# A decoder layer on one core: the down projection's weight operands made one to three products later

## The chip, the core and the metric

The kernel runs on one core of a Trainium2 chip. The metric is the device time of one execution in microseconds (us). Its engines are PE (TensorE, matmuls), DVE (VectorE), ACT (ScalarE), POOL (GpSimd) and SP (SyncE, here only a DMA queue); each works through its own list of instructions in order, and they wait for one another by semaphores.

## What is computed

One decoder layer for 1056 positions (1024 of a prompt, 32 of samples), d_model 1024, all in float32:

```
x = x + 1/2 * SwiGLU_1(RMSNorm(x))          # (silu(h @ w_gate) * (h @ w_up)) @ w_down, d_ff 2816
z = RMSNorm(x) @ w_in                       # attention head group and short-conv head group
x = x + concat([attn_out, conv_out]) @ w_out
x = x + 1/2 * SwiGLU_2(RMSNorm(x))
x = x + sigmoid(RMSNorm(x) @ w_ple_gate) * (p @ w_ple_proj)
```

The change is in the product with `w_down`, which occurs twice (two down stages).

## The kernel before

**Precision.** Each float32 operand is held as a high part (a cast to the PE's reduced format, on ACT) and a low part (operand minus high part, on DVE); a product is three matmuls: high by high, low by high, high by low. `split` (L370 the cast, L371 the subtraction) makes both parts of one operand.

**Seven products.** Every 2x2 block product of the SwiGLU stages is done with seven products in place of eight; sums and differences of blocks are their operands. Products carry the numbers 1 to 7. The operands of the weights' side are 1, 2 and 4 (blocks as they are loaded, tiles `dr`) and 3, 5, 6, 7 (sums of blocks, tiles `dws`, which POOL makes in four additions, L829 to L832, in the order of operands 5, 6, 7, 3). `vh` and `vl` are the high and the low part, one place of each for every operand number: the parts of the next weights overwrite those in use, so they can be made only when the product that reads them is done.

**Flushes.** A down stage is 17 flushes (table `FLUSH`): one row of weights, one to three pairs of d_ff blocks, added to x. The positions come in two chunks, so each flush has two halves, called here the first half (chunk 0) and the second (chunk 1), with the same weights. A product in a half is three matmuls for each pair: three, six or nine.

**Order in a half.** `segment(q, p)` interleaves a half with the late products of the half before it. The seven steps are products 1, 5 of this half, 7 of the previous, 2, 6 of this, 3, 4 of the previous. After each product `out1` to `out7` take the sum from PSUM into x ("puts": L871 on DVE; L869 on ACT for part of the puts of flushes that begin with pair 0). After product 1 one put, after 5 none, after 7 two, after 2, 6, 3 and 4 one each. Products 1, 6, 7 and 4 of a half add up in one PSUM bank, 5 and 3 in a second, 2 alone in a third; there are five banks. Two waits follow: product 3 may add to its bank only after the second put of product 7 has read it, two steps after product 7; and product 5 of a half takes the bank that product 3's put of the half before it has emptied, two steps after that product.

**Who sets the order.** From the end of the gate-up stage to the end of the down stage the order on each engine is as written (`in_order`). In the second half of each flush, `follow` holds the next weights, and `step` splits operand o of them right after product o of the flush in use and its put. The additions for them (`sums`) stand at the start of the second half on POOL, whose list also holds the loads of the pairs' operands (L907) and the additions of the residual (L914, two in eight of the flushes). Flushes 5 and 6 also make the last pair's operands (`hop_last`, tiles `hd`, `hta`, `htb`, `hhi`, `sgl`), one task after each step.

In the program's steps:

```
            self.product(o, ps, o in (1, 5, 2))
            getattr(self, f"out{o}")()
            if self.follow:
                self.follow.split(o)
```

Of the kernel before, what the change touches and what calls it, by code (L numbers as in the profile page):

```python
# [78 lines left out]
FLUSH = [  # L79
    (0, 0, 1), (1, 0, 2), (2, 0, 2), (3, 0, 3), (0, 1, 4), (1, 2, 5), (2, 2, 5), (3, 3, 6), (0, 4, 7),  # L80
    (1, 5, 8), (2, 5, 8), (3, 6, 9), (0, 7, 9), (1, 8, 11), (2, 8, 11), (3, 9, 11), (0, 9, 11),
]
# [19 lines left out]
def tile_decoder_layer(  # L102
# [17 lines left out]
    def at(name, o, n, dt=F32, rows=P):  # L120

        assert o + n <= ARENA
        key = (name, o, n)
        if key not in placed:
            placed[key] = nc.alloc_sbuf_tensor_at(f"{name}_a{o}", [P, n], dt, offset=base + 4 * o).ap()
        return placed[key][:rows]
# [14 lines left out]
    def psb(pool=None):  # L141
        return (pool or mm).tile([P, 512], F32, name="ps", tag="ps")
# [27 lines left out]
    def pump_dma():  # L170
        while st["dma"] < st["end"] and st["dma"] < st["split"] + RAW:
            i = st["dma"]
            t = at("wraw", 30624 if i in (0, 26) else (URAW2 if 4 <= i < 26 else URAW)[i % 2], 1024)
            nc.sync.dma_start(out=t, in_=units[i])
            raws[i] = t
            st["dma"] += 1

    def split_one():
        i = st["split"]
        pump_dma()  # L180
        raw = raws.pop(i)
        hi = at("whi", unit_at(i), 1024, F32R)
        lo = at("wlo", unit_at(i) + 1024, 1024, F32R)
        nc.scalar.copy(out=hi, in_=raw)
        nc.vector.tensor_tensor(out=lo, in0=raw, in1=hi.bitcast(F32), op=ALU.subtract)  # L185
        parts[i] = (hi, lo)
        st["split"] += 1
        pump_dma()
# [174 lines left out]
    OPS = (1, 5, 2, 6, 7, 3, 4)  # L363
# [12 lines left out]
    def wload(gu, j):  # L376
        r = []
        for i in range(4):
            t = at("wr", WRAW + 512 * (wn_[0] % 6), 512)
            wn_[0] += 1  # L380
            nc.sync.dma_start(out=t, in_=gu[j, i])
            r.append(t)
        return r
# [4 lines left out]
    class Weights:  # L388


        def __init__(self, gu, j):
            r = wload(gu, j)
            s = [at("ws", WS + 512 * i, 512) for i in range(4)]
            add = nc.gpsimd.tensor_tensor
            add(out=s[0], in0=r[2], in1=r[3], op=ALU.add)  # L395
            add(out=s[1], in0=s[0], in1=r[0], op=ALU.add)
            add(out=s[2], in0=r[0], in1=r[2], op=ALU.add)
            add(out=s[3], in0=s[1], in1=r[1], op=ALU.add)
            self.of = {1: r[0], 2: r[1], 3: s[3], 4: r[3], 5: s[0], 6: s[1], 7: s[2]}
            self.w = {}  # L400
# [35 lines left out]
    class Quad:  # L436


        pops = 2

        def __init__(self, w, c):
            self.w, self.ch, self.follow = w, c, None

            self.then = {}
# [11 lines left out]
        def step(self, o):  # L456
            if o == 1:
                self.b = psb()
            elif o == 5:
                self.c = psb()  # L460
            elif o == 2:
                self.a = psb()
            ps = self.b if o in (1, 6, 7, 4) else self.c if o in (5, 3) else self.a
            self.product(o, ps, o in (1, 5, 2))
            getattr(self, f"out{o}")()
            if self.follow:
                self.follow.split(o)
            for fn in self.then.get(o, ()):
                fn()
            for _ in range(self.pops):  # L470
                if hops:
                    hops.pop(0)()

    hops = []

    def segment(q, p):

        for o, of in ((1, q), (5, q), (7, p), (2, q), (6, q), (3, p), (4, p)):
            if of:
                of.step(o)  # L480
# [60 lines left out]
    def hop_last(pr, c, src):  # L541


        cell = {}
        e0 = at("sgl", LASTAT, HH, F32R)

        def parts(u, n, hi, t, neg=False):
            split(hi, t.bitcast(F32R), t, neg)
            for part, v in enumerate((hi.bitcast(F32), t)):
                if n == 1:  # L550
                    nc.sync.dma_start(out=hop[pr, u, :, part * HC + c * HH:part * HC + (c + 1) * HH], in_=v)
                else:
                    nc.sync.dma_start(out=hop_dst(pr, c, u, n, part), in_=v)

        new = lambda: wtile("hhi", shape=[P, 2, HH], dt=F32R)
        return hop_sums(cell, src) + [
            lambda: parts(1, 2, new(), cell["s"][1]),
            lambda: parts(0, 1, e0, cell["s"][0][:, 0]),
            lambda: parts(3, 2, new(), cell["a"]),
            *[lambda: None] * 5,  # L560
            lambda: parts(5, 2, new(), cell["b"], True),
        ]
# [6 lines left out]
    def from_hd(pr, c):  # L569
        t = [tmp3("hd0"), tmp3("hd1")]  # L570
        for i in range(2):
            nc.sync.dma_start(out=t[i].rearrange("p i t -> p (i t)"), in_=hd[(2 * pr + i) % 16, :, c * HC:(c + 1) * HC])
        return lambda: t
# [171 lines left out]
    def gate_up(gu, g, lw, steps, down):  # L745
# [11 lines left out]
        n1 = len(bg)  # L757
        lead[1] = lead_weights(gu, 1)
        run(0, 0, -(-n1 // 8))
        run(1, 0, -(-n1 // 8))  # L760
        while bg:
            bg.pop(0)()
# [3 lines left out]
        for kp in range(2):  # L766
            bg.append(lambda kp=kp: n_t5(1, kp))
        run(0, 1)
        lead[2] = lead_weights(gu, 2)
        run(1, 1)  # L770
# [73 lines left out]

    class DownQuad(Quad):
        pops = 1

        def __init__(self, w, c, flush, done):
            super().__init__(w, c)
# [48 lines left out]
    class Down:  # L898
# [26 lines left out]
        def run(self, prev):  # L925
            w = self.w[0]
            last_use = {}
            for i, (row, p0, p1) in enumerate(FLUSH):
                for pr in range(p0, p1):
                    last_use[pr] = i  # L930
            last_row = {f[0]: i for i, f in enumerate(FLUSH)}
            for i, f in enumerate(FLUSH):
                nxt = None
                for c in range(2):
                    if c and i + 1 < len(FLUSH):
                        nxt = self.w[i + 1]
                        nxt.sums()
                    done = (lambda r=f[0], c=c: self.hook(r, c)) if last_row[f[0]] == i and f[0] else None
                    q = DownQuad(w, c, f, done)
                    if c:  # L940
                        q.follow = nxt
                        if i in (0, 2):
                            for o in UNITS:
                                q.then[o] = [lambda pr=2 + i // 2, o=o: self.load(pr, o)]
                        for pr in range(f[1], f[2]):
                            if last_use[pr] == i and pr + 4 < PAIRS:
                                for o in UNITS:
                                    q.then.setdefault(o, []).append(lambda pr=pr, o=o: self.load(pr + 4, o))
                    if i in (4, 5) and c:
                        src = from_hd(10, i - 4)  # L950
                    if i in (5, 6) and c == 0:
                        hops.extend(hop_last(10, i - 5, src))
                    if i == len(FLUSH) - 1 and c:
                        q.then[2] = [split_one]
                    if c == 0:
                        res = [self.residual(m, RES[i][1]) for m in (RES[i][0], RES[i][0] + 4)] if i in RES else []
                    else:
                        for fn in res:
                            fn()
                    segment(q, prev)  # L960
                    prev = q
                    if c and i + 2 < len(FLUSH):
                        self.w[i + 2] = self.weights(i + 2)
                    if (i, c) in ((len(FLUSH) - 2, 1), (len(FLUSH) - 1, 0)):
                        st["end"] = self.end - 3 * c
                        pump_dma()
                w = nxt
            segment(None, prev)
            self.hook(0, 0)
            split_one()  # L970
            self.hook(0, 1)
# [172 lines left out]
    for h in range(8):  # L1144
        o = h * TBL
# [586 lines left out]
```

## Time and profile before

| | |
|---|---|
| median of 3 runs | 2020.54 us (2017.55 to 2022.1) |
| the profiled execution | 2018.56 us, its span 2016.8 us |
| granted clock, mean over the span | 0.984 of full speed |
| busy share of the span | PE 97%, DVE 68%, POOL 46%, ACT 38% |
| matmuls of the two down stages | 2 x 1848 (L860 to L862) |
| casts and subtractions for the down weights | 238 each |

PE is busy nearly throughout. A row of a timeline shows in brackets how long the engine was idle before it, and what ended that.

### The profile page before, as it was taken

The numbers are of one execution on the slowest core, as the hardware profiler recorded it, in microseconds if no ns is written. First come the engines' busy times: TensorE is split into PE (matmuls) and PEld (weight loads), VectorE is DVE, ScalarE is ACT, GpSimd is POOL, SyncE is SP. The second block draws the span as 40 slices with busy tenths as digits, with TensorE's granted clock in tenths as the row PEclk, the third lists the DMA queues.
The fourth block names the chain that finished last, engine by engine and source line by source line (L and its number), as shares of the span: only waits on it lengthen the run. The fifth ranks groups of instructions, "written<-read, shape, count | busy, mean of one in ns | idle before, by whom it ended". The sixth has DMA issues, their size and how long they took to land. (4 is left out here: it accounts for less than half of the span.)

```text
span 2016.8 us, 38417 instructions
## 1 busy us (share of the span) xinstructions
PE 1947.3 (97%) x14639; PEld 1892.7 (94%) x14639; DVE 1378.3 (68%) x2572; ACT 770.8 (38%) x1654; POOL 918.1 (46%) x911
## 2 busy tenths in 40 slices
PE   7999999999999999999998899999999999999999
PEld 6999999999999998999886899999999999999898
DVE  6848877777577766366675367687777765777764
ACT  5324444444432234323343133344444434322431
POOL 2426654655566645012222025375565555675500
PEclk8999999999999999999998899999999999999999
DMA  7225754454999724201002321465444369876232
GB/s 253 74 75 194 246 167 139 136 163 135 316 321 322 252 81 152 68 23 43 26 29 75 117 97 54 140 221 169 134 156 160 124 216 326 295 262 233 67 111 88
DMA packets 189549, 315.47 MB, mean 156 GB/s; under 512 B 20801, under 2 KB 121545, under 8 KB 189236
## 3 DMA queue, kind: packets, MB, share of 16 engines
q1 hardware_dynamic: 164852, 224.55, 34.2%
q0 software_dynamic: 23648, 87.28, 12.8%
q8 instruction: 115, 1.88, 0.4%
q10 hardware_dynamic: 864, 1.18, 0.2%
q14 instruction: 70, 0.57, 0.1%
HBM read 204.66 MB, written 109.99 MB: 156 GB/s over the span
## 5 line engine op out<-in xcount | busy, mean ns | idle before, releaser
L452 PE MATMUL ps<-bh_a,wh_a 128*128 128x264 f32 x2128 | 603.3, 285 | 3.7 <-DVE u L604 1.8
L453 PE MATMUL ps<-bh_a,wl_a 128*128 128x264 f32 x2128 | 603.8, 284 | 0.0
L454 PE MATMUL ps<-bl_a,wh_a 128*128 128x264 f32 x2128 | 599.5, 284 | 0.0
L452 PEld LDWEIGHTS ps<-bh_a,wh_a 128*128 128x128 f32 x2128 | 399.1, 188 | 6.7 <-DVE g_a L607 2.5
L453 PEld LDWEIGHTS ps<-bh_a,wl_a 128*128 128x128 f32 x2128 | 400.0, 188 | 0.0
L454 PEld LDWEIGHTS ps<-bl_a,wh_a 128*128 128x128 f32 x2128 | 399.7, 189 | 0.0
L860 PE MATMUL ps<-pair_a,vh_a 128*128 128x264 f32 x1232 | 356.1, 289 | 25.8 <-DVE x_a L871 24.2
L862 PE MATMUL ps<-pair_a,vh_a 128*128 128x264 f32 x1232 | 351.8, 286 | 0.0
L861 PE MATMUL ps<-pair_a,vl_a 128*128 128x264 f32 x1232 | 350.9, 285 | 0.0
L860 PEld LDWEIGHTS ps<-pair_a,vh_a 128*128 128x128 f32 x1232 | 233.2, 189 | 34.0 <-ACT vh_a L370 12.3
L871 DVE SCALAR_TENSOR_TENSOR x_a<-ps,x_a 128x264 f32<-128x264 f32 x412 | 170.3, 426 | 104.2 <-PE ps L862 79.9
L861 PEld LDWEIGHTS ps<-pair_a,vl_a 128*128 128x128 f32 x1232 | 233.4, 189 | 0.0
L862 PEld LDWEIGHTS ps<-pair_a,vh_a 128*128 128x128 f32 x1232 | 232.7, 189 | 0.0
L342 PE MATMUL ps<-xnh_a,whi_a 128*128 128x384 f32 (+1 forms) x528 | 175.4, 332 | 9.4 <-DVE x_a L1551 6.0
L343 PE MATMUL ps<-xnh_a,wlo_a 128*128 128x384 f32 (+1 forms) x528 | 173.2, 328 | 1.6 <-DVE wlo_a L185 1.6
L344 PE MATMUL ps<-xnl_a,whi_a 128*128 128x384 f32 (+1 forms) x528 | 172.5, 327 | 0.0
L371 DVE TENSOR_TENSOR wl_a<-ws_a,wh_a 128x512 fp32r<-128x512 f32 x152 | 132.1, 869 | 35.9 <-ACT wh_a L370 35.5
L395 POOL TENSOR_TENSOR ws_a<-wr_a,wr_a 128x512 f32<-128x512 f32 x38 | 51.1, 1345 | 224.9 <-DMA wr_a<-in_w2gu_dram 88.4
L370 ACT CAST vh_a<-dws_a 128x384 fp32r<-128x384 f32 (+2 forms) x136 | 63.7, 468 | 201.0 <-PE ps L862 177.7
L370 ACT CAST wh_a<-ws_a 128x512 fp32r<-128x512 f32 x152 | 94.3, 620 | 101.4 <-PE ps L454 87.6
L907 POOL DMA_DIRECT2D pair_a<-hop x154 | 82.8, 544 | 84.0 <-PE ps L862 76.2
L371 DVE TENSOR_TENSOR wl_a<-wr_a,wh_a 128x512 fp32r<-128x512 f32 x114 | 108.1, 949 | 12.6 <-ACT wh_a L370 11.6
(268 smaller groups left out, 4177.3 us busy)
## 6 DMA issues: line engine op xcount, KB each, us to landing
pair_a<-hop POOLq DMA_DIRECT2D x154, 528.0 KB, 7.5
hop<-sg_a SPq DMA_DIRECT2D x240, 264.0 KB
wr_a<-in_w1gu_dram SPq DMA_DIRECT2D x88, 256.0 KB
wr_a<-in_w2gu_dram SPq DMA_DIRECT2D x88, 256.0 KB
hop<-sge_a SPq DMA_DIRECT2D x80, 132.0 KB
wraw_a<-in_win_dram SPq DMA_DIRECT2D x18, 512.0 KB
dr_a<-in_w1d_dram SPq DMA_DIRECT2D x44, 192.0 KB
dr_a<-in_w2d_dram SPq DMA_DIRECT2D x44, 192.0 KB
```

What stands on the lines that cost most here:

```text
L342: nc.tensor.matmul(ps[:, :W], lhsT=wh, rhs=xh, start=(k == 0), stop=False)
L343: nc.tensor.matmul(ps[:, :W], lhsT=wl, rhs=xh, start=False, stop=False)
L344: nc.tensor.matmul(ps[:, :W], lhsT=wh, rhs=xl, start=False, stop=(k == n - 1))
L370: nc.scalar.copy(out=hi, in_=src)
L371: nc.vector.tensor_tensor(out=lo, in0=src, in1=hi.bitcast(F32), op=ALU.subtract)
L452: nc.tensor.matmul(ps[:, :HH], lhsT=wh[:, ks], rhs=bh, start=(start and k == 0), stop=False, skip_group_check=True)
L453: nc.tensor.matmul(ps[:, :HH], lhsT=wl[:, ks], rhs=bh, start=False, stop=False, skip_group_check=True)
L454: nc.tensor.matmul(ps[:, :HH], lhsT=wh[:, ks], rhs=bl, start=False, stop=last, skip_group_check=True)
L860: nc.tensor.matmul(ps[:, :HH], lhsT=wh[:, ks], rhs=bh, start=(start and i == 0), stop=False, skip_group_check=True)
L861: nc.tensor.matmul(ps[:, :HH], lhsT=wl[:, ks], rhs=bh, start=False, stop=False, skip_group_check=True)
L862: nc.tensor.matmul(ps[:, :HH], lhsT=wh[:, ks], rhs=bl, start=False, stop=(i == n - 1), skip_group_check=True)
L871: nc.vector.scalar_tensor_tensor(out=x, in0=ps[:, :HH], scalar=f, in1=x, op0=ALU.mult, op1=ALU.add)
```

## The change

An operand's split is no longer called at once but put on a list, `behind`, with the number of the step at which it is due; the list is worked off in its order after each step's put. Outside the down stage the delay is 0 steps. In the down stage it is 1 step for operands 1, 7 and 3, 2 steps for 5, 2 and 4, and 3 for 6, but 0 for those of the last flush. Steps of the next half count, so operand 6, split after step 5 of the second half before, is split after step 1 of the next first half; 7 and 3 move within that half, to its steps 4 and 7; and operand 4 moves from its end to step 2 of the following second half, just ahead of operand 1 of the weights after.

```
@@ class Quad
+        behind = {o: 0 for o in OPS}
@@ Quad.step
             if self.follow:
-                self.follow.split(o)
+                behind.append((steps[0] + self.behind[o], lambda: self.follow.split(o)))
+            while behind and behind[0][0] <= steps[0]:
+                behind.pop(0)[1]()
+            steps[0] += 1
...
+    behind, steps = [], [0]
@@ class DownQuad(Quad)
+        behind = {1: 1, 5: 2, 2: 2, 6: 3, 7: 1, 3: 1, 4: 2}
@@ Down.run
+                    if i == len(FLUSH) - 2 and c:
+                        q.behind = Quad.behind
```

The lists of PE, POOL and SP hold the same instructions in the same order as before; those of ACT and DVE are in another order, with the same instructions.

In the listings, `x_a<-ps` is a put, and the low parts have the endings `vl_a_6049` operand 1, `6066` 5, `6105` 2, `6122` 6, `6188` 7, `6217` 3, `6235` 4. First DVE from the end of flush 12's first half to the start of flush 13, in the first down stage, before:

```order
L371 TENSOR_TENSOR vl_a_6217<-dws_a_6021,vh_a_6216 128x256
L871 SCALAR_TENSOR_TENSOR x_a_72<-ps,x_a_72 128x264
L371 TENSOR_TENSOR vl_a_6235<-dr_a_6291,vh_a_6234 128x256
L871 SCALAR_TENSOR_TENSOR x_a_72<-ps,x_a_72 128x264
L371 TENSOR_TENSOR vl_a_6049<-dr_a_6026,vh_a_6048 128x384
L371 TENSOR_TENSOR vl_a_6066<-dws_a_6018,vh_a_6065 128x384
L871 SCALAR_TENSOR_TENSOR x_a_72<-ps,x_a_72 128x264 x3
L371 TENSOR_TENSOR vl_a_6105<-dr_a_6028,vh_a_6104 128x384
L871 SCALAR_TENSOR_TENSOR x_a_72<-ps,x_a_72 128x264
L371 TENSOR_TENSOR vl_a_6122<-dws_a_6019,vh_a_6121 128x384
L871 SCALAR_TENSOR_TENSOR x_a_72<-ps,x_a_72 128x264 x5
```

and now:

```order
L371 TENSOR_TENSOR vl_a_6217<-dws_a_6021,vh_a_6216 128x256
L878 SCALAR_TENSOR_TENSOR x_a_72<-ps,x_a_72 128x264
L371 TENSOR_TENSOR vl_a_6235<-dr_a_6289,vh_a_6234 128x256
L371 TENSOR_TENSOR vl_a_6049<-dr_a_6026,vh_a_6048 128x384
L878 SCALAR_TENSOR_TENSOR x_a_72<-ps,x_a_72 128x264 x3
L371 TENSOR_TENSOR vl_a_6066<-dws_a_6018,vh_a_6065 128x384
L878 SCALAR_TENSOR_TENSOR x_a_72<-ps,x_a_72 128x264 x2
L371 TENSOR_TENSOR vl_a_6105<-dr_a_6028,vh_a_6104 128x384
L878 SCALAR_TENSOR_TENSOR x_a_72<-ps,x_a_72 128x264 x2
L371 TENSOR_TENSOR vl_a_6122<-dws_a_6019,vh_a_6121 128x384
```

Ahead of the row of three puts (7, 7, 2) of the second half stood 4, 1 and 5, and stand 3, 4 and 1; ahead of the put of product 3 (the last before `6122` moved away) stood 2 and 6 as well, and stands only 5.

DVE in the first half of flush 5, before (the first row ends with the two puts of product 7):

```order
L871 SCALAR_TENSOR_TENSOR x_a_72<-ps,x_a_72 128x264 x5
L371 TENSOR_TENSOR vl_a_6188<-dws_a_6020,vh_a_6187 128x384
L371 TENSOR_TENSOR hd_6812<-hd_6812,hhi 128x528
L871 SCALAR_TENSOR_TENSOR x_a_72<-ps,x_a_72 128x264
L371 TENSOR_TENSOR hd_6811<-hd_6811,sgl_a_6906 128x264
L871 SCALAR_TENSOR_TENSOR x_a_72<-ps,x_a_72 128x264
L371 TENSOR_TENSOR hta<-hta,hhi 128x528
L871 SCALAR_TENSOR_TENSOR x_a_72<-ps,x_a_72 128x264
L371 TENSOR_TENSOR vl_a_6217<-dws_a_6021,vh_a_6216 128x384
```

and now:

```order
L878 SCALAR_TENSOR_TENSOR x_a_72<-ps,x_a_72 128x264 x2
L371 TENSOR_TENSOR hd_6810<-hd_6810,hhi 128x528
L878 SCALAR_TENSOR_TENSOR x_a_72<-ps,x_a_72 128x264
L371 TENSOR_TENSOR vl_a_6188<-dws_a_6020,vh_a_6187 128x384
L371 TENSOR_TENSOR hd_6809<-hd_6809,sgl_a_6904 128x264
L878 SCALAR_TENSOR_TENSOR x_a_72<-ps,x_a_72 128x264
L371 TENSOR_TENSOR hta<-hta,hhi 128x528
L878 SCALAR_TENSOR_TENSOR x_a_72<-ps,x_a_72 128x264 x2
L371 TENSOR_TENSOR vl_a_6217<-dws_a_6021,vh_a_6216 128x384
```

The subtraction of operand 7 (`6188`) went from ahead of the first task on `hd` to behind it and the put that follows; operand 3's (`6217`) went behind one more put.

DVE in the second half of flush 0, before:

```order
L371 TENSOR_TENSOR vl_a_6235<-dr_a_5891,vh_a_6234 128x128
L371 TENSOR_TENSOR vl_a_6049<-dr_a_6026,vh_a_6048 128x256
L371 TENSOR_TENSOR vl_a_6066<-dws_a_6018,vh_a_6065 128x256
L871 SCALAR_TENSOR_TENSOR x_a_72<-ps,x_a_72 128x264 x2
L371 TENSOR_TENSOR vl_a_6105<-dr_a_6028,vh_a_6104 128x256
```

and now:

```order
L371 TENSOR_TENSOR vl_a_6235<-dr_a_5891,vh_a_6234 128x128
L371 TENSOR_TENSOR vl_a_6049<-dr_a_6026,vh_a_6048 128x256
L878 SCALAR_TENSOR_TENSOR x_a_72<-ps,x_a_72 128x264 x2
L371 TENSOR_TENSOR vl_a_6066<-dws_a_6018,vh_a_6065 128x256
L878 SCALAR_TENSOR_TENSOR x_a_72<-ps,x_a_72 128x264
```

Only operand 5 (`6066`) moved here, from ahead of the two puts (7 and 2) to behind them, since the operands split in the last gate-up step are not delayed.

## Rows read from the trace of the kernel before

**Rows 1.** Head of the page.

```profile
span 2016.8 us, 38417 instructions
```

**Rows 2.** Windows of the two down stages (busy us, instructions, granted clock, DMA).

```profile
517.00:768.00 251.00, 238.25 (x1889) 234.20 (x1889) 176.88 (x343) 83.63 (x187) 149.90 (x174) 0.99 0.73 248
1660.00:1910.00 250.00, 236.92 (x1898) 232.78 (x1897) 177.36 (x344) 84.25 (x189) 150.41 (x175) 1.00 0.72 241
```

**Rows 3.** Waits of PE: who for whom, us in total, times, longest.

```profile
PE ps L860 <- DVE x_a L871: 24.2, 24, 2.9
```

**Rows 4.** Timeline of PE: start, us, form, [idle before <- its end].

```profile
527.00 0.39 PE L860 MATMUL ps<-pair_a,vh_a 128*128 128x264 f32 x1 [1.77 <-DVE x_a L871]
...
592.94 0.36 PE L860 MATMUL ps<-pair_a,vh_a 128*128 128x264 f32 x1 [0.89 <-DVE x_a L871]
...
597.55 0.36 PE L860 MATMUL ps<-pair_a,vh_a 128*128 128x264 f32 x1 [1.10 <-DVE x_a L871]
...
658.79 0.28 PE L860 MATMUL ps<-pair_a,vh_a 128*128 128x264 f32 x1
...
660.07 0.36 PE L860 MATMUL ps<-pair_a,vh_a 128*128 128x264 f32 x1
...
672.68 0.36 PE L860 MATMUL ps<-pair_a,vh_a 128*128 128x264 f32 x1 [0.30 <-DVE x_a L871]
...
701.63 0.36 PE L860 MATMUL ps<-pair_a,vh_a 128*128 128x264 f32 x1 [1.30 <-DVE x_a L871]
...
705.32 0.36 PE L860 MATMUL ps<-pair_a,vh_a 128*128 128x264 f32 x1 [0.91 <-DVE x_a L871]
...
717.19 0.36 PE L860 MATMUL ps<-pair_a,vh_a 128*128 128x264 f32 x1 [0.66 <-ACT vh_a L370]
...
748.83 0.56 PE L860 MATMUL ps<-pair_a,vh_a 128*128 128x264 f32 x1 [2.94 <-DVE x_a L871]
...
1769.36 0.36 PE L860 MATMUL ps<-pair_a,vh_a 128*128 128x264 f32 x1 [0.47 <-DVE x_a L871]
```

**Rows 5.** Timeline of DVE, second half of flush 12, start of 13.

```profile
697.05 1.03 DVE L371 TENSOR_TENSOR vl_a<-dr_a,vh_a 128x256 fp32r<-128x256 f32 x1
...
699.30 1.37 DVE L371 TENSOR_TENSOR vl_a<-dws_a,vh_a 128x384 fp32r<-128x384 f32 x1
...
700.60 1.23 DVE L871 SCALAR_TENSOR_TENSOR x_a<-ps,x_a 128x264 f32<-128x264 f32 x3
...
701.74 1.48 DVE L371 TENSOR_TENSOR vl_a<-dr_a,vh_a 128x384 fp32r<-128x384 f32 x1
...
703.49 1.34 DVE L371 TENSOR_TENSOR vl_a<-dws_a,vh_a 128x384 fp32r<-128x384 f32 x1
...
704.75 1.10 DVE L871 SCALAR_TENSOR_TENSOR x_a<-ps,x_a 128x264 f32<-128x264 f32 x3
```

**Rows 6.** Timeline of DVE, second half of flush 0.

```profile
525.66 0.94 DVE L371 TENSOR_TENSOR vl_a<-dws_a,vh_a 128x256 fp32r<-128x256 f32 x1
526.53 0.76 DVE L871 SCALAR_TENSOR_TENSOR x_a<-ps,x_a 128x264 f32<-128x264 f32 x2
```

**Rows 7.** Timeline of DVE, around the start of flush 10's second half.

```profile
666.40 0.56 DVE L371 TENSOR_TENSOR vl_a<-dws_a,vh_a 128x384 fp32r<-128x384 f32 x1 [0.17 <-ACT vh_a L370]
```

**Rows 8.** Timeline of POOL, the same place.

```profile
667.10 1.01 POOL L832 TENSOR_TENSOR dws_a<-dws_a,dr_a 128x384 f32<-128x384 f32 x1 [2.11 <-issue]
```

**Rows 9.** Timeline of DVE, first half of flush 5.

```profile
583.03 0.66 DVE L371 TENSOR_TENSOR vl_a<-dws_a,vh_a 128x384 fp32r<-128x384 f32 x1
...
584.33 0.71 DVE L371 TENSOR_TENSOR hd<-hd,hhi 128x528 fp32r<-128x528 f32 x1 [0.65 <-POOL htb L511]
...
586.60 0.42 DVE L871 SCALAR_TENSOR_TENSOR x_a<-ps,x_a 128x264 f32<-128x264 f32 x1
```

**Rows 10.** Windows, 5 us after the longest wait of the first stage.

```profile
749.00:754.00 5.00, 5.00 (x23) 5.00 (x24) 3.45 (x9) 2.06 (x4) 0.72 (x2) 0.50 0.02 3
```

**Rows 11.** Timeline of POOL, second half of flush 12.

```profile
698.92 1.34 POOL L831 TENSOR_TENSOR dws_a<-dr_a,dr_a 128x384 f32<-128x384 f32 x1
```

## The prediction

> **What bounds the kernel now.** I read the page's head first, then the windows of the two down stages, the waits of PE, and only then timelines at single starts of PE. The reader is to see four things. The profiled execution took 2018.56 us, of which the span is 2016.8 [rows 1]; 1.76 us lie around it. In the two down stages PE is busy 238.25 of 251 us and 236.92 of 250 [rows 2]: 12.8 and 13.1 us are idle, 25.8 in all, and more than that the change can hardly give back. Of this, 24.2 us in 24 waits end with a put on DVE [rows 3]. These waits are not spread evenly; they are a dozen late starts a stage, of 0.3 to 2.9 us [rows 4]. DVE itself is busy 177 of 250 us [rows 2], so it is late at places and idle at others, and what counts is the order of its list. The granted clock is 0.99 and 1.00 in these windows [rows 2].
>
> The late starts are of two kinds. A: product 3 of a first half, in step 6 of the second half, waits for product 7's second put. B: product 5 at a half's second step waits for the put of product 3 of the half before.
>
> **The change part by part.** No instruction is added or removed; PE, POOL and SP keep their lists. So there is no new work, and the sum is over waits.
>
> *Casts on ACT.* A cast can run once the old product has ended and ACT has reached it. ACT is busy 84 of 250 us [rows 2], so most casts still run when they do now. I count the casts at nothing; the cover is ACT's idle time. The exceptions are flushes in which ACT also does puts or the next stage's norm; there a cast that now stands behind such work comes later, and with it its subtraction, by one such ACT instruction or two. The subtractions of operands 2 and 6 have three steps or more until their product, 3.3 us with three pairs (a matmul is 236.92/1898 = 0.125 us of PE [rows 2], a step of nine 1.12), and I count nothing for them either.
>
> *Kind B.* At the start of flush 13, DVE does operand 2 (701.74, 1.48 us), a put, operand 6 (703.49, 1.34), and then at 704.75 three puts, the first of which is product 3's [rows 5]. That one ends near 705.2, and product 5 starts at 705.32 after 0.91 us idle [rows 4]. With the change only operand 5 stands between put 2 and this put, where 2 and 6 stood: the put comes 1.3 us earlier, more than the 0.91 that PE waited. Late next is operand 2, needed two steps after; it follows the put, and 1.5 us fit. Gain 0.9 a stage, 1.8 in two. At the starts of flushes 5, 9 and 10 the same wait is small: product 5 starts 1.28 us after product 1 (at flush 10, 658.79 to 660.07 [rows 4]), 0.16 more than nine matmuls. Three a stage, 0.16 each: 1.0 in two stages.
>
> *Kind A, first flush.* Operand 5 (525.66, 0.94 us) ends just as the puts begin at 526.53 [rows 6]; it moves behind them. PE idles 1.77 us there [rows 4]; 0.8 of it goes, 1.6 in two stages. What stays is operand 1, still ahead of the puts.
>
> *Kind A, elsewhere.* This is where I expect little. Ahead of the puts of product 7 three subtractions follow one another now (4, 1, 5), and three will then (3, 4, 1). At flush 12 the last of them (699.30) holds the puts at 700.60 [rows 5], and PE idles 1.30 [rows 4]: unchanged. Two kinds of flush differ. Where POOL's four additions come early, the fourth starts at 667.10 [rows 8], 0.14 us after operand 3's subtraction ends at 666.96 [rows 7]; in the code it overwrites the block that this one reads. Delayed, the subtraction runs with POOL waiting for it, 0.56 us alone [rows 7] in place of 1.03 beside POOL [rows 5]: about 0.45 less ahead of the puts. That is flushes 10 and 13, with 0.30 and 0.66 idle [rows 4] (the second row names ACT, but by the code that product waits for the put): 0.3 and 0.4, 1.4 in two stages. And in flush 7 of the second stage, where PE idles 0.47 at 1769.36 [rows 4], operand 5 waits for POOL's late first addition and will stand behind the puts: 0.5.
>
> *A cost: flush 5.* Operand 7 now runs at 583.03, 0.66 us, while DVE would wait anyway: the next task on hd waits 0.65 us for POOL until 584.33 [rows 9]. It moves behind that wait. The put of product 3 at 586.60 [rows 9] moves with it, by 0.55 us at least, and by up to 1.0 if the task before it falls beside POOL's first addition. Product 5 of the second half, on time now, then starts late. Bounds: nothing, if the idle 0.89 us at 592.94 [rows 4] takes it up, and 1.0 if the later DMA chain also delays the start at 597.55, which idles 1.10 now [rows 4] and would otherwise gain. I take 0.6 a stage, 1.2 in two.
>
> *Not touched.* The largest wait, 2.94 us at 748.83 [rows 4], stands in flush 15, whose splits for the last flush have delay 0. In the 5 us after it the granted clock is 0.50 [rows 10], 1.2 GHz, where the stage has 0.99 and the second stage 1.00 [rows 2]. That is 1% of 251 us, about 2.5 us, which may go in the first stage or come in the second; counted at nothing, kept in the range.
>
> Gains 1.8 + 1.0 + 1.6 + 1.4 + 0.5 = 6.3, cost 1.2, sum 5.1 us. 2018.56 - 5.1 = 2013.5 for a profiled execution; it stands 1.98 us below the median of the runs, so the median becomes 2020.54 - 5.1 = 2015.4 us.
>
> **A rule that speaks against it.** At 699.30 a subtraction takes 1.37 us [rows 5], and it ends at 700.67, 0.41 us after POOL's addition from 698.92 ended at 700.26 [rows 11]; alone one takes 0.56 [rows 7]. The Trainium skill, page SBUF — State Buffer, section "Who interferes with whom", says that a VectorE instruction with two SBUF inputs and a GpSimd instruction that reads SBUF use one shared read interface, and that the later one is blocked until the first has ended. By this rule the trace agrees: the subtraction waits for one addition and then needs 0.41. The rule makes the shift of operand 3 a loss wherever POOL's additions begin with the second half, and the sum above has that in no term; it is the rival below.
>
> **The rivals.**
> *Slower: operand 3 falls beside POOL.* At present it is done at the end of the first half, alone, for 0.56 us [rows 7]; it moves behind the put of product 4, where POOL's additions run, and 1.03 [rows 5] becomes its price. The two subtractions behind it then meet the third and the fourth addition. Put 7 comes 0.47 us later in some seven flushes a stage, 14 x 0.47 = 6.6 us; with flush 5's upper end, 2.0, and the gains of kind B and of the first flush, 4.4, that is 4.2 slower: 2024.7. Against it: three subtractions stand ahead of the puts either way, and operand 4, whose place 3 takes, pays the POOL price now (697.05, 1.03 us [rows 5]). It decides once put 7 ends later than two steps after product 7.
> *It does not do what it says.* The second half keeps five subtractions, as the listing shows: 3, 4, 1, 5, 2 for 4, 1, 5, 2, 6. Kind A stays, kind B is shifted to product 2, flush 5 costs its 2.0: a gain of 0 to 3, 2019 us. For it: the wait at flush 12 is three subtractions on both sides.
> *More goes than I count.* If all DVE waits but the two of 2.94 went, 24.2 - 5.9 = 18.3 [rows 3, 4], 2002.2; half of it, 2011.4. For it: casts stop being waited for everywhere. Against it: the count ahead of put 7.
>
> **How the numbers follow.** My forecast 0.57, own range 2011.5 to 2018.5; more than that 0.10; nothing much 0.22; slower 0.11. What can be told from no change here is about 0.2%, 4 us: faster means under 2016.5. Of my forecast three fifths lie below it (0.36) and the rest just above; with 0.10 and 0.04 of the others, 0.50. Slower is 0.10, the same 0.40. The range 2008 to 2022 leaves out the far half of the larger gain and most of the slower case.
>
> **What would show it.** Right: in both stages the idle of about 0.9 at flush 13's product 5 is gone, the one in the first flush is near 1.0, the ones at flush 12 and 15 are as they were, and product 5 in flush 5's second half starts late. Wrong: the sum of DVE's waits on L860 stays over 22 us, or falls under 12; new waits of PE for `vl` at products 2 or 6; a rise of idle at product 3 in flushes 4, 8, 9 and 11, which have none now.

## The result, and the profile after

The changed kernel took 2005.79 us (median of 4 runs, 2004.25 to 2008.8), the one before 2021.26 in the same set; the ratio is 0.9927 (95% interval 0.9911 to 0.9943). Predicted were 2015.4 and a range of 2008 to 2022: the direction is right, the time lies below the range, and the gain in this set, 15.5 us, is three times the 5.1 predicted; in the stages that the change touches it is 11.5.

Where it went is seen best in the two down stages, each measured from its first matmul to the start of its last (1848 matmuls). Before they took 250.39 and 248.18 us, 498.57 together; after 244.87 and 242.20, 487.07: 11.5 us less. The span became 13.1 shorter; the other 1.6 lie where the lists are unchanged. A second set of runs of the changed kernel (below) had the same stages and a median of 2011.69.

The head of the page after, as [rows 1]:

```profile
span 2003.6 us, 38390 instructions
```

The windows of the two stages, columns as in [rows 2]. PE is idle for 9.9 and 9.1 us where it was for 12.8 and 13.1; why the stages gained more than the 6.8 between these is told further down, under idle times:

```profile
516.00:762.00 246.00, 236.07 (x1894) 233.26 (x1894) 177.72 (x343) 82.84 (x188) 150.38 (x174) 0.99 0.74 254
1653.00:1896.00 243.00, 233.87 (x1892) 231.26 (x1891) 175.45 (x342) 82.53 (x188) 151.03 (x174) 1.00 0.73 247
```

The waits of PE that answer to [rows 3] (L867 and L878 are L860 and L871 of before). Six waits and 5.3 us are gone; the longest is still there:

```profile
PE ps L867 <- DVE x_a L878: 18.9, 18, 3.1
```

Six of the late starts of PE after, first stage, to be held against [rows 4]:

```profile
525.85 0.39 PE L867 MATMUL ps<-pair_a,vh_a 128*128 128x264 f32 x1 [0.91 <-DVE x_a L878]
...
545.54 0.39 PE L867 MATMUL ps<-pair_a,vh_a 128*128 128x264 f32 x1 [0.55 <-DVE x_a L878]
...
586.66 0.39 PE L867 MATMUL ps<-pair_a,vh_a 128*128 128x264 f32 x1 [1.01 <-DVE x_a L878]
...
595.53 0.36 PE L867 MATMUL ps<-pair_a,vh_a 128*128 128x264 f32 x1 [0.92 <-DVE x_a L878]
...
698.53 0.36 PE L867 MATMUL ps<-pair_a,vh_a 128*128 128x264 f32 x1 [1.17 <-DVE x_a L878]
...
744.16 0.36 PE L867 MATMUL ps<-pair_a,vh_a 128*128 128x264 f32 x1 [3.11 <-DVE x_a L878]
```

In order: product 3 in the first flush (1.77 became 0.91), in flush 2, product 5 in flush 5's second half (new, as predicted), product 5 in flush 6, product 3 in flush 12 (1.30 became 1.17) and in flush 15 (2.94 became 3.11). The waits at flushes 10 and 13 have no row any more. Among those not shown are product 5 in flush 6's second half (0.38, new) and product 3 in flush 14 (0.67, before 0.53).

DVE at the start of flush 13, which answers to [rows 5]: ahead of the row of 700.05, which begins with product 3's put, stands one subtraction where two were, and that put comes on time.

```profile
697.50 1.23 DVE L878 SCALAR_TENSOR_TENSOR x_a<-ps,x_a 128x264 f32<-128x264 f32 x3
698.64 1.48 DVE L371 TENSOR_TENSOR vl_a<-dws_a,vh_a 128x384 fp32r<-128x384 f32 x1
700.05 0.76 DVE L878 SCALAR_TENSOR_TENSOR x_a<-ps,x_a 128x264 f32<-128x264 f32 x2
```

DVE in the first flush, as [rows 6]: the puts come ahead of operand 5.

```profile
525.37 0.76 DVE L878 SCALAR_TENSOR_TENSOR x_a<-ps,x_a 128x264 f32<-128x264 f32 x2
526.05 0.95 DVE L371 TENSOR_TENSOR vl_a<-dws_a,vh_a 128x256 fp32r<-128x256 f32 x1
```

DVE in flush 5, as [rows 9]. Operand 7 (583.36) stands behind the task on `hd`, and the task on `hta` now falls beside POOL's first addition and takes 1.76, so that product 3's put begins in the row of 586.19:

```profile
582.39 0.71 DVE L371 TENSOR_TENSOR hd<-hd,hhi 128x528 fp32r<-128x528 f32 x1 [1.27 <-POOL htb L517]
...
583.36 0.55 DVE L371 TENSOR_TENSOR vl_a<-dws_a,vh_a 128x384 fp32r<-128x384 f32 x1
...
584.51 1.76 DVE L371 TENSOR_TENSOR hta<-hta,hhi 128x528 fp32r<-128x528 f32 x1
586.19 0.76 DVE L878 SCALAR_TENSOR_TENSOR x_a<-ps,x_a 128x264 f32<-128x264 f32 x2
```

The prediction has no term for the second halves of flushes 1 and 2. In flush 1, first stage, operands 4 and 1 took 1.83 us together on DVE, beside POOL's additions, and then came operand 5 (0.96 us); after, POOL's first addition comes 2.7 us into the half where it came 0.1, and the two take 0.76, alone. Before, then after:

```profile
532.96 1.83 DVE L371 TENSOR_TENSOR vl_a<-dr_a,vh_a 128x256 fp32r<-128x256 f32 x2
```

```profile
532.53 0.76 DVE L371 TENSOR_TENSOR vl_a<-dr_a,vh_a 128x256 fp32r<-128x256 f32 x2 [0.31 <-ACT vh_a L370]
```

The second half of flush 2. DVE there before, second stage, then POOL: operands 4 and 1 run beside POOL's first additions, then operand 5 (1688.94) has to, and only at 1690.23 come the puts, 4.4 us after the half's start.

```profile
1686.76 2.26 DVE L371 TENSOR_TENSOR vl_a<-dr_a,vh_a 128x256 fp32r<-128x256 f32 x2 [0.53 <-PE ps L862]
1688.94 1.36 DVE L371 TENSOR_TENSOR vl_a<-dws_a,vh_a 128x384 fp32r<-128x384 f32 x1
1690.23 0.76 DVE L871 SCALAR_TENSOR_TENSOR x_a<-ps,x_a 128x264 f32<-128x264 f32 x2
```

```profile
1686.43 1.02 POOL L829 TENSOR_TENSOR dws_a<-dr_a,dr_a 128x384 f32<-128x384 f32 x1 [7.07 <-DMA dr_a<-in_w2d_dram]
```

And DVE after: the half starts at 1677.83, the puts come 3.3 us later, and operand 5 (1681.81) behind them; POOL's first addition comes 1.8 us into the half, where it came 0.6.

```profile
1679.49 1.72 DVE L371 TENSOR_TENSOR vl_a<-dr_a,vh_a 128x256 fp32r<-128x256 f32 x2 [0.31 <-ACT vh_a L370]
1681.13 0.76 DVE L878 SCALAR_TENSOR_TENSOR x_a<-ps,x_a 128x264 f32<-128x264 f32 x2
1681.81 0.69 DVE L371 TENSOR_TENSOR vl_a<-dws_a,vh_a 128x384 fp32r<-128x384 f32 x1
```

### The profile page after: what moved, and what is told of

Same layout as the page of the kernel before. It is cut to its first block, busy times and chain, and to the rows that moved or that the text cites. A ratio compares the mean times of both kernels' runs of the same rounds, so it can differ in the third digit from the quotient of the medians.

```text
span 2003.6 us, 38390 instructions
## 1 busy us (share of the span) xinstructions
PE 1944.0 (97%) x14639; PEld 1892.6 (94%) x14639; DVE 1378.6 (69%) x2572; ACT 768.5 (38%) x1654; POOL 921.0 (46%) x911
## 5 line engine op out<-in xcount | busy, mean ns | idle before, releaser
L867 PE MATMUL ps<-pair_a,vh_a 128*128 128x264 f32 x1232 | 354.5, 288 | 19.1 <-DVE x_a L878 18.9
L867 PEld LDWEIGHTS ps<-pair_a,vh_a 128*128 128x128 f32 x1232 | 232.7, 189 | 24.5 <-ACT vh_a L370 11.6
L878 DVE SCALAR_TENSOR_TENSOR x_a<-ps,x_a 128x264 f32<-128x264 f32 x412 | 170.4, 427 | 87.6 <-PE ps L869 75.9
```

The lines of the kernel that those rows point to most:

```text
L867: nc.tensor.matmul(ps[:, :HH], lhsT=wh[:, ks], rhs=bh, start=(start and i == 0), stop=False, skip_group_check=True)
L878: nc.vector.scalar_tensor_tensor(out=x, in0=ps[:, :HH], scalar=f, in1=x, op0=ALU.mult, op1=ALU.add)
```

## The experiments

"Stages" is the two down stages together, measured as above in one profiled execution, "rest" is the span less that. Before: stages 498.57, rest 1518.21.

| operands delayed, and what else | median us | ratio to before (95%) | stages | rest |
|---|---|---|---|---|
| all (the change) | 2005.79 | 0.9927 (0.9911 to 0.9943) | 487.07 | 1516.6 |
| the change, again | 2011.69 | 0.9954 (0.9940 to 0.9967) | 487.19 | 1520.2 |
| 5, 2, 6 | 2005.28 | 0.9911 (0.9897 to 0.9924) | 481.65 | 1519.1 |
| 2, 6 | 2022.46 | 1.0000 (0.9987 to 1.0014) | 498.46 | 1518.3 |
| 5 | 2011.54 | 0.9949 (0.9936 to 0.9961) | 489.07 | 1516.7 |
| 7, 3, 4, 1 | 2034.46 | 1.0058 (1.0045 to 1.0072) | 513.19 | 1519.2 |
| 1, 2, 6 (5 in its old place) | 2015.02 | 0.9968 (0.9958 to 0.9979) | 490.95 | 1520.2 |
| all, last flush too | 2006.11 | 0.9919 (0.9905 to 0.9932) | 484.15 | 1519.1 |
| 5, 2, 6, last flush too | 1996.29 | 0.9877 (0.9865 to 0.9890) | 476.43 | 1517.6 |
| the same, again | 2000.43 | 0.9897 (0.9876 to 0.9917) | 479.22 | 1519.2 |
| 5, 2, 6, both `htb` tasks later | 2000.95 | 0.9904 (0.9891 to 0.9917) | 479.88 | 1518.0 |
| 5, 2, 6, last flush, both tasks | 1998.67 | 0.9886 (0.9872 to 0.9900) | 476.21 | 1520.7 |
| 5, 2, 6, last flush, first task | 1991.80 | 0.9860 (0.9838 to 0.9882) | 474.02 | 1515.9 |

**Operands 5, 2 and 6 alone.**

```
-        behind = {1: 1, 5: 2, 2: 2, 6: 3, 7: 1, 3: 1, 4: 2}
+        behind = {1: 0, 5: 2, 2: 2, 6: 3, 7: 0, 3: 0, 4: 0}
```

> Only operands 5, 2 and 6 are delayed (2, 2 and 3 steps); 1, 7, 3 and 4 are made where they were before. Theory C (count): what matters is only how many subtractions stand ahead of a put; taking 5 from ahead of product 7's puts ends kind A, taking 2 and 6 from ahead of product 3's put ends kind B, and moving 3, 4 and 7 gives nothing or costs. Now only 4 and 1 stand ahead of the puts of 7, one less than in the changed kernel, so this must be faster than it: flush 12's wait (1.45 us there) falls under 0.5 in each stage, flush 5's new late start of 0.15 goes; 2003, against 2005.8 for the changed kernel. Rival P (place): kind A went because operand 3 moved to where it does not stand in the way of POOL's additions; then kind A is back in flushes 1, 2, 7, 10 and 13 (about 6 us in the two stages) and the time is about 2012.

The stages are 5.4 shorter than with the whole change, and kind A did not come back, at flushes 10 and 13 either, though operand 3 stands in its old place: theory P falls. (The median is only 0.5 lower; its rest was 2.5 longer.) Flush 12 is 1.1 shorter in each stage. DVE there has two subtractions ahead of the puts, and the three puts of 697.41 come 2.8 us after the half's start at 694.57, where they came after 4.0:

```profile
695.12 1.06 DVE L371 TENSOR_TENSOR vl_a<-dr_a,vh_a 128x256 fp32r<-128x256 f32 x1
...
696.45 1.03 DVE L371 TENSOR_TENSOR vl_a<-dr_a,vh_a 128x384 fp32r<-128x384 f32 x1
697.41 1.23 DVE L878 SCALAR_TENSOR_TENSOR x_a<-ps,x_a 128x264 f32<-128x264 f32 x3
```

**Operands 2 and 6 alone** (`5: 0` in addition).

> Only operands 2 and 6 are delayed; 5 stands ahead of product 7's puts again, 3, 4, 7 and 1 are as before. Theory C: kind B alone goes (flush 13's product 5 by 1.15 a stage, the small ones at 5, 8, 9, 10 by 0.1 to 0.25), kind A stays: about 4 us less than before, 2017; flush 12's 1.3 us and the first flush's 1.8 us are there. Rival P expects the same 2017. A third, D (backlog): product 3's puts were late mainly through the backlog that kind A leaves; then kind B does not go by this alone and the time is within 2 us of before.

Nothing, as only theory D has it, but not for its reason. Kind B did go: the first half of flush 13 is 1.15 shorter in each stage, those of flushes 5, 8, 9 and 10 by 0.1 to 0.27. Part of it came back right behind, as kind A: the second half of flush 13 is 0.67 longer in the first stage and 0.23 in the second. In the second half of flush 13 operand 5 (716.03) still stands ahead of the puts, beside POOL, and PE waits 1.32 us for them where it waited 0.66 [rows 4]; DVE first, then PE:

```profile
714.77 1.34 DVE L371 TENSOR_TENSOR vl_a<-dr_a,vh_a 128x384 fp32r<-128x384 f32 x1
716.03 1.67 DVE L371 TENSOR_TENSOR vl_a<-dws_a,vh_a 128x384 fp32r<-128x384 f32 x1
717.63 1.57 DVE L878 SCALAR_TENSOR_TENSOR x_a<-ps,x_a 128x264 f32<-128x264 f32 x4
```

```profile
718.66 0.36 PE L867 MATMUL ps<-pair_a,vh_a 128*128 128x264 f32 x1 [1.32 <-DVE x_a L878]
```

Products 5 and 3 wait one behind the other for the same list: PE that is let through at product 5 is early at product 3.

More of it, 0.97 and 0.76 us, was lost in the second halves of flush 1, and 1.5 in the second stage in the two halves before (flush 0's second, flush 1's first), where the clock fell (last section). In flush 1 operand 5 is ahead of the puts, and POOL's first addition, which it needs, now starts 2.9 and 2.3 us into the half where it started 0.1 and 0.5. The last load that it needs is issued right behind operand 2's subtraction (which ends 11.36 us into the first stage and ended at 10.55; the issues stand at 11.45 and 10.63), since by the code it overwrites the block that this one reads. In the three kernels that leave operand 2 in place this addition starts 14.9 to 15.4 us into the stage, in all others 15.9 to 18.6. The issue is 0.8 us later and the addition 2.8; where the other 2.0 come from stays open. PE there:

```profile
538.10 0.39 PE L867 MATMUL ps<-pair_a,vh_a 128*128 128x264 f32 x1 [1.31 <-DVE x_a L878]
```

**Operands 7, 3, 4 and 1 alone** (`{1: 1, 5: 0, 2: 0, 6: 0, 7: 1, 3: 1, 4: 2}`).

> The other part alone: operands 7, 3, 4 and 1 are delayed (1, 1, 2 and 1 steps), 5, 2 and 6 are not. Ahead of product 7's puts stand four subtractions now: 3, 4, 1, 5. Theory C: slower than before; the second halves of flushes 8 to 14, which have three pairs, pay up to one subtraction beside POOL each, 0.5 to 1.0 us, and flush 5 its late start: 5 to 8 us more, 2026 to 2029. Rival P: kind A goes for the same reason as in the changed kernel, 5 us less than before, 2016.

Theory C's sign, and more than its size: 14.6 us in the stages. Flushes 4, 8 and 9, on time before, each lose 1.1 us a stage, as at flush 8:

```profile
644.23 0.36 PE L867 MATMUL ps<-pair_a,vh_a 128*128 128x264 f32 x1 [0.88 <-DVE x_a L878]
```

Kind B went at flushes 5, 9 and 10 (0.25 to 0.27 each) without 2 or 6 having moved, and at flush 13 in the second stage (1.06) but not in the first (0.10 longer): PE that is late at product 3 is mostly no longer early at product 5.

**Operand 5 alone** (`{1: 0, 5: 2, 2: 0, 6: 0, 7: 0, 3: 0, 4: 0}`).

> Operand 5 alone is delayed, by 2 steps; 2 and 6 are made where they were before, so that 5, 2 and 6 now stand ahead of product 3's put, where before stood 2 and 6. Delaying 2 and 6 alone gave nothing (2022.5 against 2022.3), all three 2005.3. Theory S (sum of two): kind A goes with operand 5, but kind B grows by part of a subtraction (0.5 to 1.0 us) in the flushes with three pairs, so of the 17 us only 6 to 10 are got: 2012 to 2016. Rival F (operand 5 is all): DVE has slack behind product 7's puts, product 5 waits no longer than before, and the time is 2005 to 2009.

Theory S. Kind A is gone at all its places but flush 15 and what stays of it in the first flush (0.9), and kind B has grown, in flush 13 from 0.91 to 2.17 us:

```profile
703.26 0.36 PE L867 MATMUL ps<-pair_a,vh_a 128*128 128x264 f32 x1 [2.17 <-DVE x_a L878]
```

So 5 alone gives 9.5 in the stages, 2 and 6 alone 0.1, the three 16.9: the second part is worth 7.4 once the first is there.

**Operand 1 in operand 5's place.** Is it the number of subtractions or which ones?

```
-            while behind and behind[0][0] <= steps[0]:
-                behind.pop(0)[1]()
+            for b in [b for b in behind if b[0] <= steps[0]]:
+                behind.remove(b)
+                b[1]()
...
+        behind = {1: 3, 5: 0, 2: 2, 6: 3, 7: 0, 3: 0, 4: 0}
```

> As the run with 5, 2 and 6 delayed (2005.3), but with 1 and 5 changing places: operand 5 stays ahead of product 7's puts and operand 1 goes behind them (3 steps); the list is worked off by due step, not in its order, for that. The number of subtractions ahead of those puts is the same as there. Theory C (count): only the number counts, the time is 2005 and the two stages take 482 us, as there. Theory W (what it waits for): operand 5's subtraction needs POOL's first addition of the same half and its cast, operand 1's a block that was loaded long ago; then kind A comes back where that addition is late: product 3 starts late again in flushes 1, 2 and 7 (0.3 to 1.1 us each), and in 14 and 15, some 5 to 9 us more in the two stages: 488 us, 2011.

Theory W: 490.95 against 481.65 with as many subtractions ahead of the puts. Of the 9.3 the largest piece, 2.8, lies in the second halves of flush 1, where POOL's addition is late, and 1.4 lie in flush 14. Another 2.5 lie in two first halves of the second stage (flushes 1 and 16) in which the granted clock is 0.73 and 0.76, so that some 6.8 are left for the exchange itself. Not all of theory W's places show it: flush 2 and flush 15's wait are as with 5, 2 and 6 to 0.14 us, and flush 7 only in the second stage (0.3). Against the kernel before, which has one subtraction more there, this run's stages are 7.6 shorter: the number counts as well. The rows of flush 1 (lines are one higher here), of POOL, ACT, DVE and PE, one after the other: the addition waits for the weights' transfer, the cast for the addition, the subtraction 3.43 us for the cast, the puts (539.35) for the subtraction, and PE for the puts.

```profile
537.62 0.72 POOL L836 TENSOR_TENSOR dws_a<-dr_a,dr_a 128x256 f32<-128x256 f32 x1 [4.22 <-DMA dr_a<-in_w1d_dram]
```

```profile
538.38 0.40 ACT L370 CAST vh_a<-dws_a 128x256 fp32r<-128x256 f32 x1 [3.01 <-POOL dws_a L836]
```

```profile
538.82 0.61 DVE L371 TENSOR_TENSOR vl_a<-dws_a,vh_a 128x256 fp32r<-128x256 f32 x1 [3.43 <-ACT vh_a L370]
539.35 0.76 DVE L879 SCALAR_TENSOR_TENSOR x_a<-ps,x_a 128x264 f32<-128x264 f32 x2
```

```profile
539.83 0.39 PE L868 MATMUL ps<-pair_a,vh_a 128*128 128x264 f32 x1 [1.94 <-DVE x_a L879]
```

**The change, with the last flush delayed too.**

```
-                        q.behind = Quad.behind
+                        q.behind = {1: 0, 5: 2, 2: 2, 6: 2, 7: 0, 3: 0, 4: 0}
```

> The changed kernel, with the last flush's operands 5, 2 and 6 delayed too (by 2, 2 and 2 steps), where the changed kernel has no delay. There operand 5's subtraction, at 742.59 in the changed kernel, waits for POOL and holds product 7's puts until 743.12, and product 3 starts 3.39 us after its predecessor. Theory C: the puts then follow operand 1 at about 741.5, product 3 starts some 2 us earlier in each stage, and the low clock behind the wait may go as well: 4 to 6 us less than the changed kernel, about 2001. Rival L (POOL late): the additions for the last flush are late whatever DVE does, and the wait only moves to product 5 of flush 16: within 1.5 us of the changed kernel, 2005.

By the stages between the two. The wait in flush 15 falls from 3.11 to 1.45 us, and flush 16 pays 0.94 at product 6, for which product 1's put (in the row of 751.48) stands behind a subtraction whose cast comes after the norm's work on ACT; the stages are 2.9 shorter. The median does not show it. PE, then DVE:

```profile
746.47 0.36 PE L867 MATMUL ps<-pair_a,vh_a 128*128 128x264 f32 x1 [1.45 <-DVE x_a L878]
...
752.04 0.36 PE L867 MATMUL ps<-pair_a,vh_a 128*128 128x264 f32 x1 [0.94 <-DVE x_a L878]
```

```profile
750.90 0.65 DVE L371 TENSOR_TENSOR vl_a<-dws_a,vh_a 128x256 fp32r<-128x256 f32 x1 [0.51 <-ACT vh_a L370]
751.48 1.23 DVE L878 SCALAR_TENSOR_TENSOR x_a<-ps,x_a 128x264 f32<-128x264 f32 x3
```

**5, 2 and 6, with the last flush** (`{5: 2, 2: 1, 6: 1}` there, the others 0).

> Operands 5, 2 and 6 delayed as in the run with these three alone (2005.3), and in the last flush too, by 2, 1 and 1 steps, so that 2 and 6 are made before the next stage's norm begins on ACT. Theory G (given back): in the run that delayed the last flush by 2, 2 and 2 the wait in flush 15 got about 1.7 us shorter, but product 6 of flush 16 came 1.1 us late, since its operand's cast stood behind the norm's work on ACT and product 1's put behind that subtraction; with 1 and 1 this late start goes: the two down stages get 3 to 4 us shorter than with the three alone (481.65 us together), the time 2001 to 2003. Rival L (POOL late): what is won in flush 15 is lost again in flush 16 in some other wait, the stages get less than 1.5 us shorter, 2005.

The stages get 5.2 shorter than with the three alone, the time 9.0: theory G, though a rest of 0.5 and 0.46 us of idle stays in flushes 15 and 16 (rows below). From flush 15 on the gain is 4.7 us, in the repeat below 4.8; 3.7 of it lie in the first stage, where the low clock behind the wait is gone too.

```profile
739.64 0.36 PE L867 MATMUL ps<-pair_a,vh_a 128*128 128x264 f32 x1 [0.50 <-DVE x_a L878]
...
742.52 0.36 PE L867 MATMUL ps<-pair_a,vh_a 128*128 128x264 f32 x1 [0.46 <-DVE x_a L878]
```

**The task on `htb` three steps later.**

```
-            *[lambda: None] * 5,
+            *[lambda: None] * 8,
```

> Operands 5, 2 and 6 delayed as in the run with these three alone; and the last task of the last pair's operands (the split of htb) comes three steps later, after product 4 of flush 5's second half. In the run with the three alone the second half of flush 5 got 1.1 us shorter and the first half of flush 6 0.6 to 1.2 us longer: the cast of htb on ACT waits 5.4 to 6.1 us for a transfer to end (at 75.8 and 75.1 us of the stage, whatever came before), and product 3's put stands behind its subtraction on DVE. Theory T (transfer): with the task behind that put, product 5 of flush 6 starts on time, 1.5 to 2.5 us less in each stage, 3 to 5 in all, 2001. Rival M (moves): the puts behind the task come late instead, products 6 or 3 of flush 6 wait, and less than 1 us is won.

Theory T holds at its place: flush 6's first half falls by 2.4 and 1.8 us. With operands 5, 2 and 6 alone product 5 waited there 2.30 us, because the cast on ACT waited for a transfer; the two rows are ACT's and DVE's of that run:

```profile
594.68 0.64 ACT L367 ACTIVATE hhi<-htb 128x528 fp32r<-128x528 f32 x1 [6.07 <-DMA hop<-hd]
```

```profile
595.36 0.71 DVE L368 SCALAR_TENSOR_TENSOR htb<-htb,hhi 128x528 fp32r<-128x528 f32 x1 [3.80 <-ACT hhi L367]
```

But flush 8 loses 1.1 and 1.7, since POOL's first addition for it, in flush 7's second half, waits for the weights' load (this run's row of POOL):

```profile
623.95 1.01 POOL L835 TENSOR_TENSOR dws_a<-dr_a,dr_a 128x384 f32<-128x384 f32 x1 [6.23 <-DMA dr_a<-in_w1d_dram]
```

**Both edits.**

> The two preceding edits together on operands 5, 2 and 6 delayed. If both theories (G and T) hold, the gains add up, since the places lie 70 us apart: 6 to 8 us less than with the three alone, 1997 to 1999. By the rivals 2004.

The median lies in the expected range, but the stages, 476.2, do not add up: 5.4 us less than with the three alone, where the parts gave 5.2 and 1.8. Flush 8 of the second stage alone lost 2.2.

**Both edits, but only the first of the two `htb` tasks moved** (`* (8 - 3 * c)`).

> Operands 5, 2 and 6 delayed, the last flush by 2, 1 and 1, and the task on htb three steps later only for the first half's pair (in flush 5), not for the one in flush 6. With both tasks later, flush 6 won 1.8 to 2.4 us a stage and flush 8 lost 1.1 to 2.2 in three stages of four, where POOL's additions waited for the weights' load until 6.2 us after it was free. Theory Q: that load is late because of the second task alone; then flush 8 is on time and the two stages take 473 us, against 476.4 and 476.2 for the two parents. Rival N: flush 8 is late again, or (6, 1) takes it up, and the stages stay at 476.

Theory Q for the most part: 474.0; flush 8 is on time in the second stage and 0.5 late in the first. With 1991.8 us it is the shortest of all the kernels run.

**Two kernels again, unedited.**

> The changed kernel once more, unedited. Of the 13.1 us between the two profiles the down stages have 11.5; the other 1.6 lie where all lists are the same as before. Theory R (run to run): the two stages take 487 us again to within 1 us, the time outside them varies by 2 us and more, so the 1.6 is not the change's. Rival E (elsewhere): the rest of the span is again 1.5 us shorter than in the kernel before, to within 0.5.

> Operands 5, 2 and 6 delayed and the last flush by 2, 1 and 1, once more and unedited (1996.3 before), since the changed kernel came to 2005.8 in one set of runs and 2011.7 in another: the stages take 476.4 us again to within 1 us, and the time shows how far the rest of the program moves it, 1994 to 2002.

The changed kernel's stages came back to 0.12 us, its rest was 3.6 longer: theory R. In the fourteen profiles of this study the first down stage begins at 514.6 to 521.2 us, though all lists are alike up to there. The second kernel's stages were 2.8 longer than the first time, more than expected. Of this 1.6 is the first half of flush 6 in the first stage: PE waits there about as long as the first time (2.11 and 2.03 us), but then the granted clock falls and is 0.85 over the half, where it was 1.00. So a difference of 3 us between two kernels here is read from their stages, not from one median.

## Why the prediction was right or wrong

Terms of the sum, both stages together, against the lengths of the halves in the two profiles:

| term | predicted | measured |
|---|---|---|
| kind B, flush 13 | -1.8 | -2.3 |
| kind B, small (5, 9, 10; also 8) | -1.0 | -1.8 |
| kind A, first flush | -1.6 | -1.4 |
| kind A, flushes 10 and 13 | -1.4 | -2.6 |
| kind A, flush 7 | -0.5 | -1.0 |
| kind A, flushes 1 and 2 | none | -2.0 |
| flushes 5 and 6 | +1.2 | +0.45 |
| flushes 15 and 16, clock | 0 | -0.8 |
| sum | -5.1 | -11.5 |

- **The step that failed is "Kind A, elsewhere: this is where I expect little".** It gave 5.6 us, not 1.9. It counted: three subtractions ahead of the puts before, three now. The count is right, and a fourth does cost (the run with 7, 3, 4 and 1 alone). But they are not the same three. Operand 5's needs POOL's newest addition, so it never runs before POOL's additions, and where the weights' transfer is late it holds the puts until then (row below, flush 7 of the second stage before: DVE waited 1.85 us). Operands 3, 4 and 1 need nothing of this, and run alone where POOL is late, as in flush 1. That it matters which ones stand there is shown by the run with 1 in 5's place, with two ahead instead of three. Flushes 1 and 2 had no term at all, though PE was late there before.

```profile
1767.47 0.94 DVE L371 TENSOR_TENSOR vl_a<-dws_a,vh_a 128x384 fp32r<-128x384 f32 x1 [1.85 <-ACT vh_a L370]
```

- **The reason given for flushes 10 and 13 is not needed.** It was that operand 3's subtraction, once moved, runs with POOL waiting for it. At flush 10 it did (0.55 us), at flush 13 it ran beside POOL (0.87). But the runs that move operand 5 and leave operand 3 in place gain as much there or more: 0.53 and 0.89 in the first stage, where the change gained 0.53 and 0.79.
- **Each wait that goes was taken 0.24 too small.** A matmul's row lasts 0.28 or 0.29 us and the next begins 0.12 after it (first and second row at the end of this document), and the second matmul behind a wait begins 0.2 after the first (705.32 in [rows 4], and the row below). So a start that a row calls 0.91 late costs 0.91 + 0.28 - 0.12 + 0.08 = 1.15. Flush 13's kind B (1.15), flush 10 (0.30 shown, 0.53 gone) and flush 7 (0.47 shown, 0.71 gone) are larger for this reason, and the small waits of kind B are no idle in a row at all. The sum of PE's idle times misses as much at each of its waits.

```profile
705.51 0.28 PE L861 MATMUL ps<-pair_a,vl_a 128*128 128x264 f32 x1
```

- **Kind B is right where it was put, but not a sum by itself.** Without operand 5's move the gain was lost again at other places, part of it at once as kind A (2 and 6 alone: 0.1 us in all). The prediction added the two kinds as if they were apart.
- **Flush 5**: product 5 is late as predicted (1.01 at 586.66), and it costs less, 0.16 a stage in that half: the idle 0.89 at 592.94 is gone, as the lower of the two bounds has it. In the run with 5, 2 and 6 alone that half came 1.3 us earlier and flush 6 gave 0.6 to 1.4 of it back: a part of what is won here is lost again to the transfer.
- **Right**: the first flush to 0.2 us and what stays of it (0.91, "near 1.0"); flush 12 unchanged; flush 15 not touched. The low clock there lasted shorter (0.83 over flush 16's first half, before 0.76): 0.8 of the 2.5 us kept in the range. All signs that the prediction named for being right were there, and none for being wrong; they stood at places that it had counted, so they could not tell of those that it had left out.
- **The slower rival** (operand 3 beside POOL) has a real mechanism: delaying 7, 3, 4 and 1 costs 5.4 us in the stages on top of 5, 2 and 6, of which 4.0 lie in the second halves of flushes 12 and 14. Operand 3 in flush 12 takes 1.03 us now. It is outweighed, not absent; no run moved operand 3 by itself.
- **"More goes than I count"** has the direction of the miss: the medians, 2005.79 and 2011.69, lie between its two figures or next to the lower one. But of the 18.3 us of waits only 5.3 are gone, and its reason, that casts stop being waited for, holds for operand 5's alone.
- **The rule of the Trainium skill** (SBUF — State Buffer, "Who interferes with whom") stayed true in size: three-pair subtractions that run beside POOL's additions take up to 1.7 us (716.03 with 2 and 6 alone), alone 0.55 (583.36). But it speaks for a delay as much as against: operand 5 pays it behind the puts, where PE mostly does not wait for it.
- **Outside the stages** 1.6 us of the first comparison are not the change's; by the stages the change is worth 11.5 us, and the two sets' medians, 15.5 and 9.9 apart from before, lie on both sides of that.

## What to carry to other kernels

In a list that is worked off in order, put first the instructions whose operands are long there, and put what waits for another engine's fresh result behind the instruction that the bounding engine waits for; counting how many stand ahead is not enough. Moving a reader later also moves the load that reuses its buffer. Waits that end with the same engine's list are not separate terms: take one away and see who then comes early at the next. Measure a change of half a per cent in the stage that it touches, with an unedited kernel run twice.

## What the runs showed of the hardware that was not expected

The clock fell after a wait of 1.78 us in the run with 2 and 6 alone, where waits of 1.77 and 1.78 at the same place in the two stages of the kernel before [rows 4, the first] were followed by no drop. PE in the second stage of that run, and the window after the wait: the matmuls of the last two rows start 0.24 us apart, those of the first two 0.12, at a granted clock of 0.53, nearly the lower level of 1.2 GHz, and the half of flush 1 that follows took 1.0 us longer than before. Whether a wait of this length brings the drop is not told by its length alone: in flush 15 of the kernel before a wait of 2.94 did in one stage and not in the other, and in flush 6 one of 2.11 did in the repeated run of 5, 2 and 6 with the last flush, where one of 2.30 with 5, 2 and 6 alone did not.

```profile
1667.41 0.28 PE L868 MATMUL ps<-pair_a,vl_a 128*128 128x264 f32 x1
1667.53 0.29 PE L869 MATMUL ps<-pair_a,vh_a 128*128 128x264 f32 x1
1669.60 0.44 PE L867 MATMUL ps<-pair_a,vh_a 128*128 128x264 f32 x1 [1.78 <-DVE x_a L878]
1669.84 0.42 PE L868 MATMUL ps<-pair_a,vl_a 128*128 128x264 f32 x1
```

```profile
1669.60:1673.10 3.50, 3.50 (x16) 3.50 (x17) 1.04 (x3) 0.99 (x3) 2.43 (x6) 0.53 0.98 290
```
